# Two added pairs of one-column products in a two-layer decoder trunk: one in the first feed-forward, one in the convolution

## The chip, the cores and the metric

The kernel runs on one core of a Trainium2 chip. The metric is the time of one execution in microseconds, taken on the device. A core has TensorE (matmuls, "PE" in the profile, with its weight loads listed apart as "PEld"), VectorE ("DVE"), ScalarE ("ACT"), GpSimd ("POOL") and SyncE ("SP", which here issues the loads from memory). They run beside each other and wait for each other through semaphores. On TensorE every product is two instructions: a weight load, which puts a block of up to 128 columns into the array, and a matmul, which streams the other operand through it.

## What is computed

Two decoder layers over 256 positions and a model width of 1024, all in 32-bit floating point, about 150 MB of weights read once. Layer 0 mixes by attention, layer 1 by a short gated convolution, and each then has a gated feed-forward of width 2816:

```python
for i in range(DEPTH):                                   # DEPTH = 2
    mod = sc @ w_ada[i] + b_ada[i]                       # shifts, scales, gates
    sh_m, sc_m, g_m, sh_f, sc_f, g_f = jnp.split(mod, 6, axis=-1)
    h = modulate(x, norm_mix[i], sh_m, sc_m)
    y = moba_attention(...) if i % 2 == 0 else short_conv(...)
    x = x + g_m[:, None, :] * y
    h = modulate(x, norm_ffn[i], sh_f, sc_f)
    x = x + g_f[:, None, :] * swiglu(h, w_gate_up[i], w_down[i])

def short_conv(h, w_in, conv_w, w_out):
    b_gate, c_gate, u = jnp.split(h @ w_in, 3, axis=-1)
    u = c_gate * u
    up = jnp.pad(u, ((0, 0), (2, 0), (0, 0)))
    y = sum(conv_w[j] * up[:, j:j + S] for j in range(3))
    return (b_gate * y) @ w_out

def swiglu(h, w_gate_up, w_down):
    g, u = jnp.split(h @ w_gate_up, 2, axis=-1)
    return (jax.nn.silu(g) * u) @ w_down
```

## The kernel before

**Three products for one.** Every weight and every activation is split into a rounded part and a remainder (names ending in h and l), and a block of a matrix product is summed from three matmuls in the function mm3: high by high (line 248), high by low and low by high (lines 249 and 250). In the feed-forwards, the convolution and the output projections the weights are stationary: a matmul loads a block of 128x128 weights (wh or wl) and streams 256 positions of the activations (f0h, f0l and so on). Two of three neighbouring matmuls use the same stationary block, but each loads it anew. In the key and value projections of the attention the activations are the stationary operand and the weights stream.

**Chunks.** Weights arrive in chunks of 1 MB (256 output columns of all 1024 inputs) through five buffers; ScalarE rounds a chunk into wh (line 98), VectorE takes the remainder into wl (line 99), each in two halves and through three buffers. A chunk's load and split are put into the program two chunks ahead of its use. One chunk makes 48 matmuls: eight blocks of inputs, two halves of 128 columns, three products. In between, VectorE computes the modulation of later sublayers from chunks of w_ada (line 109).

**The stages.** A sublayer starts with the function raw_gemm: its first two weight chunks are multiplied with the not yet normalised activations (tiles raw_f, raw_m, 258 columns: 256 positions and two columns for the shift), 96 matmuls, so that TensorE has work while the norm is computed. In their midst stand small products for the norm (ms_n, rr_n). After it follow the ordinary chunks through feat_gemm: in a feed-forward ten times a gate chunk (tile pg) and an up chunk (tile pu), for j = 1 to 10, and then the down projection (op_d: 8 blocks of outputs, 22 blocks of inputs, three products, 528 matmuls); in the convolution one chunk for the B gate (pb) of j = 0, then for j = 1 to 3 one chunk each for pc, pu and pb, and then the output projection (op_co, 192 matmuls).

**The pair that is already there.** raw_gemm ends with a call of settle: two matmuls with a stationary block of 128x128 ones in bf16 and one streamed column, into a PSUM tile of its own that nothing reads. There are three such pairs: settle_f in each feed-forward, settle_m in the convolution.

**What sets the order.** The first stage, up to the queries and two of the key chunks, is written out by hand. For the rest a scheduler of the framework places each engine's instructions; on TensorE it follows the program's order, apart from the small products of the norm and the attention. PSUM tiles are of three kinds: "gemm" with four buffers, "alt" and "misc" with two each; settle takes its tile from "misc".

Of the kernel before, what the change touches and what calls it, by code (L numbers as in the profile page):

```python
# [15 lines left out]
P = 128  # L16
# [17 lines left out]
def trunk_kernel(ctx: ExitStack, tc: tile.TileContext, x_t, cols_in, scale_in, shift_in, ada_in, qk_rows, kv_in, o_in,  # L34
                 in_in, out_in, gu_in, down_in, out_f):
    nc = tc.nc
# [7 lines left out]
    def ps_gemm(name):  # L44
        return psum.tile([P, 2, CW], F32, tag="gemm", name=name, bufs=4)

    def ps_misc(name):
        return psum.tile([P, 512], F32, tag="misc", name=name, bufs=2)
# [15 lines left out]
    one_b = const.tile([P, 1], BF16, name="one_b")  # L64
# [102 lines left out]
    def conv_col(j, k):  # L167
        return v_cols[:, 32 + j * KD + k:][:, :1]
# [62 lines left out]
    def produce(upto):  # L231
        while pos[0] < len(chunks) and pos[0] <= upto:
            ch = chunks[pos[0]]
            if ch[0] == "a":
                ada_piece(*ch[1:])
            else:
                ready[ch[1]] = prep(ch[2], ch[3], "_".join(map(str, ch[1])), ch[1] in first_two)
            pos[0] += 1

    def get(key):  # L240
        n = place[key]
        produce(order[min(n + AHEAD, len(order) - 1)])
        return ready.pop(key)


    def mm3(ps, lhs, rhs, first, last):
        (ah, al), (bh, bl) = lhs, rhs
        nc.tensor.matmul(ps, ah, bh, start=first, stop=False, skip_group_check=True)  # L248
        nc.tensor.matmul(ps, ah, bl, start=False, stop=False, skip_group_check=True)  # L249
        nc.tensor.matmul(ps, al, bh, start=False, stop=last, skip_group_check=True)  # L250

    def feat_gemm(parts, xs, nk):
        xh, xl = xs
        for k in range(nk):
            for ps, (wh, wl) in parts:
                for o in range(2):
                    cs = slice(o * P, (o + 1) * P)
                    mm3(ps[:, o], (wh[:, k, cs], wl[:, k, cs]), (xh[:, k], xl[:, k]),
                        k == 0 and o == 0, k == nk - 1)
# [128 lines left out]
    def split(dst, k, src, name, psum_src=False):  # L388
        nc.scalar.activation(dst[0][:, k], src, AF.Copy)
        nc.vector.tensor_sub(dst[1][:, k], src, dst[0][:, k].bitcast(F32))  # L390

    def settle(name):

        ps = ps_misc("settle_" + name)
        for i in range(2):
            nc.tensor.matmul(ps[:, i:i + 1], one_b.to_broadcast([P, P]), one_b, start=True, stop=True, skip_group_check=True)

    def raw_gemm(keys, norm, name):

# [27 lines left out]
    def ffn(l, norm, av, done):  # L427
        for j in range(KF // 2):
            if j == 0:
                (s, bs), (a, ba), hs = raw_gemm([("g", l, j), ("u", l, j)], norm, f"f{l}")  # L430
                for o in range(2):
                    nc.scalar.activation(s[:, o], s[:, o], AF.Silu, bias=bs[:, o:o + 1])
                    nc.vector.scalar_tensor_tensor(a[:, o], a[:, o], ba[:, o:o + 1], s[:, o], op0=ALU.add,
                                                   op1=ALU.mult)
            else:
                pg, pu = ps_gemm(f"pg_{l}_{j}"), ps_gemm(f"pu_{l}_{j}")
                feat_gemm([(pg, get(("g", l, j)))], hs, KD)
                feat_gemm([(pu, get(("u", l, j)))], hs, KD)
                s = tmp.tile([P, 2, S], F32, tag="s", name=f"s_{l}_{j}")
                nc.scalar.activation(s, pg, AF.Silu)  # L440
                a = tmp.tile([P, 2, S], F32, tag="a", name=f"a_{l}_{j}")
                nc.vector.tensor_mul(a, s, pu)
            split(av, slice(2 * j, 2 * j + 2), a, f"{l}_{j}")
        out_proj([[(("d", l, j, i), n) for i, n in enumerate((8, 8, 6))] for j in range(4)], av, l, G_F, done)
# [15 lines left out]
    def mod_columns(y, name):  # L460

        ps = ps_misc(f"mod_c_{name}")
        n = y.shape[1] // P
        for i in range(n):
            nc.tensor.matmul(ps[:, i:i + 1], y[:, i * P:(i + 1) * P], firsts, start=True, stop=True)
        return ps[:, :n]
# [71 lines left out]
    with tc.manual_schedule(engines={mybir.EngineType.PE, mybir.EngineType.DVE, mybir.EngineType.Activation}):  # L538
# [13 lines left out]
        for k in range(KD):  # L552
            nc.tensor.matmul(c_ps[k // 4][:, k % 4 * P:][:, :P], sc[:, k:k + 1].to_broadcast([P, P]), ident, start=True,
                             stop=True)
# [18 lines left out]
        ps = mod_columns(y, "sc0")  # L573
# [13 lines left out]
        for k in range(KD):  # L587
            n = k + 1
# [167 lines left out]
    zv, zraw = wide_pair("zv")  # L756
    n1 = Norm("n1", 1, SH_M, SC_M, zraw)
    ffn(0, n0, av, n1.take)


# [3 lines left out]
    for j in range(4):  # L764
        up = ups[j % 2]
        if j == 0:
            (cg, bc), (cu, bu), hs = raw_gemm([("cg", j), ("cu", j)], n1, "m1")
            for o in range(2):
                nc.scalar.activation(cg[:, o], cg[:, o], AF.Identity, bias=bc[:, o:o + 1])
                nc.vector.scalar_tensor_tensor(up[:, o, 2:], cu[:, o], bu[:, o:o + 1], cg[:, o], op0=ALU.add,  # L770
                                               op1=ALU.mult)
        else:
            pc, pu = ps_gemm(f"pc_{j}"), ps_gemm(f"pu_{j}")
            feat_gemm([(pc, get(("cg", j)))], hs, KD)
            feat_gemm([(pu, get(("cu", j)))], hs, KD)
            cg = tmp.tile([P, 2, S], F32, tag="s", name=f"cg_{j}")
            nc.scalar.activation(cg, pc, AF.Copy)
            with tc.high_priority(400):
                nc.vector.tensor_mul(up[:, :, 2:], cg, pu)
        pb = (ps_alt2 if j else ps_gemm)(f"pb_{j}")  # L780
        feat_gemm([(pb, get(("cb", j)))], hs, KD)
        y = tmp.tile([P, 2, S], F32, tag="a", name=f"y_{j}")
        with tc.high_priority(400):
            for o in range(2):
                k = 2 * j + o
                nc.scalar.activation(y[:, o], up[:, o, 0:S], AF.Copy, scale=conv_col(0, k))
            for i in (1, 2):
                for o in range(2):
                    nc.vector.scalar_tensor_tensor(y[:, o], up[:, o, i:i + S], conv_col(i, 2 * j + o), y[:, o],
                                                   op0=ALU.mult, op1=ALU.add)  # L790
        z = tmp.tile([P, 2, S], F32, tag="s", name=f"z_{j}")
        with tc.high_priority(400):
            nc.vector.tensor_mul(z, y, pb)
            split(zv, slice(2 * j, 2 * j + 2), z, f"z{j}")
# [6 lines left out]
    def store(k):  # L801
        if k >= KD - 2:
            nc.sync.dma_start(out_f[:, k], xT[:, k])
        elif k % 2:
            nc.sync.dma_start(out_f[:, k - 1:k + 1], xT[:, k - 1:k + 1])

    ffn(1, n2, av, store)


# [58 lines left out]
```

## Time and profile before

| | |
|---|---|
| median of three runs | 601.7 us (600.98 to 604.31) |
| the profiled execution | 601.54 us |
| its span, from the first to the last instruction | 599.8 us |
| TensorE, matmuls | busy 590.5 us, 98% of the span, 5044 in the records |
| VectorE | busy 455.2 us, 76% |
| ScalarE | busy 314.3 us, 52% |
| memory traffic | 156 MB, mean 260 GB/s |
| granted TensorE clock | 0.999 |

The profiled execution's own time is 1.74 us above its span, for what lies before the first and after the last instruction. A row of the instruction list gives a start, a duration, the engine, the line, and the tiles written and read. Matmuls are pipelined: one lasts about 0.28 us in the records, and the next starts about 0.12 us after it, so that the distance from start to start, not the duration, is what a matmul costs in a stream. A view by windows counts every instruction that reaches into a window, so the count holds two or three matmuls that only overlap its edges. A few per cent of matmul records can be missing from a trace.

### The profile page before, as it was taken

Reading aid. Unit: us, or ns where it says so; the run is one execution under the profiler, and the core shown is the slowest. Engines: PE = TensorE matmul, PEld = TensorE weight load, DVE = VectorE, ACT = ScalarE, POOL = GpSimd, SP = SyncE. Lnnn points to the kernel's source line nnn. Section 1 sums busy time; section 2 is a strip of 40 time slices with the busy share of each in tenths; the row PEclk is TensorE's granted clock in tenths of the full one; section 3 lists DMA queues with packets and bytes.
Section 4 is the critical chain, followed back from the end, with each engine's and each line's share of the span. In section 5 each row is a group of like instructions: output and inputs, shape, how many; then the busy total and the mean of one; then the engine's idle time right before and its main releaser. Section 6 shows DMA issues by size and latency. Waiting matters only on the chain.

```text
span 599.8 us, 12042 instructions
## 1 busy us (share of the span) xinstructions
PE 590.5 (98%) x5044; PEld 581.9 (97%) x5044; DVE 455.2 (76%) x719; ACT 314.3 (52%) x526; POOL 1.1 (0%) x8
## 2 busy tenths in 40 slices
PE   7999999999999999999999999999999999999997
PEld 6899999999999999999999999999999999999997
DVE  2788988998997887878878998559887566664440
ACT  3646898776644354444444744527744544443330
POOL 0000000000000000000000000000000000000000
PEclk9999999999999999999999999999999999999999
DMA  8799989856798899868996577634486675655400
GB/s 332 269 379 413 377 308 324 334 198 231 257 384 293 330 346 343 283 245 291 354 361 256 190 285 275 212 141 152 181 317 260 216 251 179 260 190 183 169 18 18
DMA packets 25109, 156.04 MB, mean 260 GB/s; under 512 B 2784, under 2 KB 3168, under 8 KB 8928
## 3 DMA queue, kind: packets, MB, share of 16 engines
q1 hardware_dynamic: 24912, 155.20, 69.8%
q8 instruction: 39, 0.64, 0.4%
q10 hardware_dynamic: 144, 0.08, 0.1%
q14 instruction: 14, 0.11, 0.1%
HBM read 154.22 MB, written 1.05 MB: 259 GB/s over the span
## 4 chain that ended last, share of the span: by engine, by line
PE 96%; ACT 2%; DMA 1%; DVE 0%; issue 0%
PE pu L249 7%; PE pu L248 7%; PE pu L250 7%; PE op_d L249 7%; PE op_d L250 7%; PE op_d L248 7%; PE pg L249 6%; PE pg L248 6%; PE pg L250 6%; PE pq L248 1%; PE op_o L248 1%; PE pq L249 1%; PE raw_f L248 1%; PE pb L248 1%; PE pb L249 1%; PE raw_f L249 1%
## 5 line engine op out<-in xcount | busy, mean ns | idle before, releaser
L109 DVE SCALAR_TENSOR_TENSOR prod<-wa,c_all 128x1024 f32<-128x1024 f32 x80 | 97.7, 1222 | 11.2 <-DMA wa<-in_ada_dram 10.0
L98 ACT ACTIVATE wh_d<-wf_d 128x1024 fp32r<-128x1024 f32 (+1 forms) x48 | 45.3, 981 | 67.0 <-issue 46.3
L99 DVE TENSOR_TENSOR wl_d<-wf_d,wh_d 128x1024 fp32r<-128x1024 f32 (+1 forms) x48 | 52.9, 1133 | 24.9 <-ACT wh_d L98 24.9
L98 ACT ACTIVATE wh_g<-wf_g 128x1024 fp32r<-128x1024 f32 x44 | 45.7, 1052 | 46.7 <-issue 46.7
L98 ACT ACTIVATE wh_u<-wf_u 128x1024 fp32r<-128x1024 f32 x44 | 44.5, 1051 | 47.9 <-issue 47.4
L99 DVE TENSOR_TENSOR wl_u<-wf_u,wh_u 128x1024 fp32r<-128x1024 f32 x44 | 52.3, 1221 | 16.4 <-ACT wh_u L98 16.3
L99 DVE TENSOR_TENSOR wl_g<-wf_g,wh_g 128x1024 fp32r<-128x1024 f32 x44 | 53.4, 1221 | 2.4 <-ACT wh_g L98 2.4
L249 PE MATMUL op_d<-a0l,wh_d 128*128 128x256 f32 x176 | 49.3, 280 | 0.0
L248 PE MATMUL op_d<-a0h,wh_d 128*128 128x256 f32 x176 | 49.1, 279 | 0.0
L250 PE MATMUL op_d<-a0h,wl_d 128*128 128x256 f32 x176 | 49.1, 279 | 0.0
L248 PE MATMUL op_d<-a1h,wh_d 128*128 128x256 f32 x176 | 48.6, 276 | 0.0
L249 PE MATMUL op_d<-a1l,wh_d 128*128 128x256 f32 x176 | 48.6, 276 | 0.0
L250 PE MATMUL op_d<-a1h,wl_d 128*128 128x256 f32 x176 | 48.6, 276 | 0.0
L249 PE MATMUL pg<-f0l,wh_g 128*128 128x256 f32 x160 | 44.8, 280 | 0.0
L249 PE MATMUL pu<-f0l,wh_u 128*128 128x256 f32 x160 | 44.8, 280 | 0.0
L248 PE MATMUL pg<-f0h,wh_g 128*128 128x256 f32 x160 | 44.7, 280 | 0.0
L250 PE MATMUL pg<-f0h,wl_g 128*128 128x256 f32 x160 | 44.6, 279 | 0.0
L248 PE MATMUL pu<-f0h,wh_u 128*128 128x256 f32 x160 | 44.6, 279 | 0.0
L250 PE MATMUL pu<-f0h,wl_u 128*128 128x256 f32 x160 | 44.6, 279 | 0.0
L248 PE MATMUL pg<-f1h,wh_g 128*128 128x256 f32 x160 | 44.2, 277 | 0.0
L249 PE MATMUL pg<-f1l,wh_g 128*128 128x256 f32 x160 | 44.2, 276 | 0.0
L250 PE MATMUL pg<-f1h,wl_g 128*128 128x256 f32 x160 | 44.2, 276 | 0.0
(297 smaller groups left out, 2031.7 us busy)
## 6 DMA issues: line engine op xcount, KB each, us to landing
wa<-in_ada_dram SPq DMA_DIRECT2D x40, 1024.0 KB, 5.8
wf_g<-in_gate_up_dram SPq DMA_DIRECT2D x22, 1024.0 KB, 4.9
wf_u<-in_gate_up_dram SPq DMA_DIRECT2D x22, 1024.0 KB, 4.9
wf_d<-in_down_dram SPq DMA_DIRECT2D x16, 1024.0 KB, 5.6
wf_d<-in_down_dram SPq DMA_DIRECT2D x8, 768.0 KB, 5.5
wa_sc<-in_scale_dram SPq DMA_DIRECT2D x8, 512.0 KB, 6.5
wa_sh<-in_shift_dram SPq DMA_DIRECT2D x8, 512.0 KB, 7.0
wf_qk<-in_qk_rows_dram SPq DMA_DIRECT2D x8, 512.0 KB, 7.3
```

What stands on the lines that cost most here:

```text
L98: nc.scalar.activation(wh[:, a:b], wf[:, a:b], AF.Copy)
L99: nc.vector.tensor_sub(wl[:, a:b], wf[:, a:b], wh[:, a:b].bitcast(F32))
L109: nc.vector.scalar_tensor_tensor(t, w, 1.0, c_all, op0=ALU.mult, op1=ALU.mult, accum_out=dst)
L248: nc.tensor.matmul(ps, ah, bh, start=first, stop=False, skip_group_check=True)
L249: nc.tensor.matmul(ps, ah, bl, start=False, stop=False, skip_group_check=True)
L250: nc.tensor.matmul(ps, al, bh, start=False, stop=last, skip_group_check=True)
```

## The change

The function settle gets a second argument, the number of stationary columns of its second product; it is 128 unless said otherwise. Two calls with 64 are added. One stands in the first feed-forward only, at j = 1, between the gate chunk and the up chunk. The other stands in the convolution at j = 1, after the B-gate chunk of j = 0 and before the first pc chunk. The three pairs inside raw_gemm stay as they are.

```diff
-    def settle(name):
+    def settle(name, m=P):
 
         ps = ps_misc("settle_" + name)
-        for i in range(2):
-            nc.tensor.matmul(ps[:, i:i + 1], one_b.to_broadcast([P, P]), one_b, start=True, stop=True, skip_group_check=True)
+        for i, n in enumerate((P, m)):
+            nc.tensor.matmul(ps[:n, i:i + 1], one_b.to_broadcast([P, n]), one_b, start=True, stop=True, skip_group_check=True)
...
                 feat_gemm([(pg, get(("g", l, j)))], hs, KD)
+                if l == 0 and j == 1:
+                    settle("u1", P // 2)
                 feat_gemm([(pu, get(("u", l, j)))], hs, KD)
...
             pc, pu = ps_gemm(f"pc_{j}"), ps_gemm(f"pu_{j}")
+            if j == 1:
+                settle("c1", P // 2)
             feat_gemm([(pc, get(("cg", j)))], hs, KD)
             feat_gemm([(pu, get(("cu", j)))], hs, KD)
```

On TensorE this is the place in the first feed-forward, between the last product of the gate chunk (tile pg_1) and the first of the up chunk (pu_1); one_b is the vector of ones:

```order
 L249 MATMUL pg_1_2004<-f0l,wh_g_1_1825 128x256
 L250 MATMUL pg_1_2004<-f0h,wl_g_1_1826 128x256
+L396 LDWEIGHTS one_b
+L396 MATMUL settle_u_2062<-one_b 128x1
+L396 LDWEIGHTS one_b
+L396 MATMUL settle_u_2062<-one_b 64x1
 L248 MATMUL pu_1_2005<-f0h,wh_u_1_1833 128x256
 L249 MATMUL pu_1_2005<-f0l,wh_u_1_1833 128x256
```

Two weight loads and two matmuls stand between products that followed each other directly before. The changed kernel's rows on TensorE in the convolution, between the B-gate chunk (pb) and the first C-gate chunk (pc):

```order
L250 MATMUL pb_4208<-m1h,wl_cb_4026 128x256
L396 LDWEIGHTS one_b
L396 MATMUL settle_c_4278<-one_b 128x1
L396 LDWEIGHTS one_b
L396 MATMUL settle_c_4278<-one_b 64x1
L248 MATMUL pc_4276<-m1h,wh_cg_4039 128x256
L249 MATMUL pc_4276<-m1l,wh_cg_4039 128x256
```

The same four rows again; no other row of TensorE, and none of the other engines, changes its place.

## The prediction

> **What bounds the kernel now.** I read the page first: the span, the engines' shares, and the chain that ended last.
>
> ```profile
> span 599.8 us, 12042 instructions
> PE 590.5 (98%) x5044; PEld 581.9 (97%) x5044; DVE 455.2 (76%) x719; ACT 314.3 (52%) x526; POOL 1.1 (0%) x8
> PE 96%; ACT 2%; DMA 1%; DVE 0%; issue 0%
> ```
>
> TensorE is the bound: 96% of the chain is its own. Then the waits of TensorE, to see whether anything holds it up where the change is made:
>
> ```profile
> PE c_ps L553 <- ACT sc L545: 1.8, 1, 1.8
> PE warm L527 <- DVE ident_r L539: 1.8, 1, 1.8
> PE pv L249 <- DVE wl_v L99: 0.6, 1, 0.6
> PE op_o L248 <- ACT ovh L389: 0.5, 1, 0.5
> ```
>
> These are the longest. All lie in the opening and the attention; in the feed-forwards and the convolution TensorE waits for nobody. There the time is the number of matmuls times the distance from one start to the next. So I took the windows view over three long steady stretches, with TensorE alone: the first feed-forward, the convolution, the second feed-forward. The columns are the window, its length, the busy time with the count of matmuls, the granted clock, the DMA share and GB/s.
>
> ```profile
> 150.00:320.00 170.00, 170.00 (x1446) 1.00 0.84 312
> 337.00:410.00 73.00, 73.00 (x622) 1.00 0.56 202
> 430.00:594.00 164.00, 164.00 (x1450) 1.00 0.54 191
> ```
>
> This is the finding on which everything rests. A matmul of 0.28 us reaches over a window's edge, so some 2.4 of each count (0.28 divided by the spacing) belong outside: 170.00/1443.6 = 117.8 ns, 73.00/619.6 = 117.8 ns, 164.00/1447.5 = 113.3 ns. The same instruction, 128x128 by 256 columns, at the same granted clock of 1.00, has **two steady spacings**, 4.5 ns apart. The first feed-forward and the convolution run at the wide one, the second feed-forward at the narrow one, and each holds its own for its whole length, over every buffer of weights. The two feed-forwards are the same program, so size, operands and buffers do not choose it. What does stands at its beginning, and the timeline of TensorE shows both beginnings, first feed-forward, then second (start, duration):
>
> ```profile
> 147.46 0.28 PE L250 MATMUL raw_f<-a0h,wl_u 128*128 128x258 f32 x1
> 147.58 0.20 PE L396 MATMUL settle_f<-one_b 128*128 128x1 bf16 x2
> 147.64 0.36 PE L248 MATMUL pg<-f0h,wh_g 128*128 128x256 f32 x1
> 147.84 0.28 PE L249 MATMUL pg<-f0l,wh_g 128*128 128x256 f32 x1
> 147.96 0.28 PE L250 MATMUL pg<-f0h,wl_g 128*128 128x256 f32 x1
> ...
> 427.31 0.28 PE L250 MATMUL raw_f<-a1h,wl_u 128*128 128x258 f32 x1
> 427.43 0.20 PE L396 MATMUL settle_f<-one_b 128*128 128x1 bf16 x2
> 427.50 0.36 PE L248 MATMUL pg<-f1h,wh_g 128*128 128x256 f32 x1
> 427.69 0.28 PE L249 MATMUL pg<-f1l,wh_g 128*128 128x256 f32 x1
> 427.81 0.28 PE L250 MATMUL pg<-f1h,wl_g 128*128 128x256 f32 x1
> ```
>
> A pair of short products interrupts the stream; the next product starts early, then waits for its weights, and the second one after the pair comes 0.20 us later in the first case, 0.19 us in the second. From then on the stream is wide in the one and narrow in the other. I read this as a lock: how weight loads and matmuls fall against each other when the stream restarts settles the spacing until something interrupts it again.
>
> **The change part by part.** It removes nothing and moves nothing. It adds two pairs, each into a stream that runs wide.
>
> *Price of a pair.* From the last product ahead of settle_f to the second one behind it pass 147.84 - 147.46 = 0.38 us, where two spacings of 0.118 would be 0.24: a pair costs 0.15 us, and this is the lower end, since both added loads and products must pass. A gain from the short products as such is excluded; they take TensorE's time. The second added load has 64 columns, which no row of the trace shows. The load timeline bounds it:
>
> ```profile
> 147.57 0.12 PEld L396 LDWEIGHTS <-one_b 128*128 128x128 bf16 x2
> 147.62 0.19 PEld L248 LDWEIGHTS pg<-f0h,wh_g 128*128 128x128 f32 x1
> 147.73 0.19 PEld L249 LDWEIGHTS pg<-f0l,wh_g 128*128 128x128 f32 x1
> ```
>
> Two loads of ones took 0.05 us to the next start, so about 0.03 each; a load of 128 columns of weights took 0.11. If the 64-column load were as slow as that, the pair would cost 0.08 more, 0.23. I take 0.17, nearer the lower end, for half of 0.11 is 0.055, some 0.02 to 0.03 above 0.03. Two pairs: 0.34 us, between 0.30 and 0.46.
>
> The Trainium skill's page "TensorE: Matmul & The Clock Gate" says under "Weight-path perf modes — Fast Weight Load (FWL) and DoubleRow" that the fast load is on only for 128 weights of a type other than FP32, and under "LDWEIGHTS (loading the stationary operand)" that a plain load takes its columns divided by 1.2 ns. By it the 64 columns would take an estimated 53 ns and the pair 0.17 us; no row here shows such a load.
>
> *What the restart is worth.* Behind the first added pair, up to the next interruption at the convolution's raw_gemm, stand 48 matmuls of pu at j = 1, 9 x 96 of j = 2 to 10, and 528 of op_d: 1440. Behind the second stand 9 x 48 = 432 and 192 of op_co: 624. If the restart falls into the narrow spacing, each saves 4.46 ns (170.00/1443.6 less 164.00/1447.5, unrounded): 6.42 us and 2.78 us. If not, it saves nothing, and only the price is left. There is no value between, unless a stream changes its spacing half way.
>
> *Does the rest keep up?* The narrow stream asks for weights 4% faster. The windows view with all engines shows the densest stretch of the first feed-forward and the same stretch of the second:
>
> ```profile
> 153.00:261.00 108.00, 108.00 (x919) 108.00 (x918) 92.52 (x122) 49.28 (x62) 0.00 (x0) 1.00 0.88 330
> 433.00:536.00 103.00, 103.00 (x911) 103.00 (x910) 69.22 (x78) 48.97 (x59) 0.00 (x0) 1.00 0.66 241
> ```
>
> VectorE is busy 92.52 of 108.00 us, DMA 0.88. A stretch shorter by 4%, 103.9 us, would need 89% and 0.92: under one, so I cost this at nothing. The cover is the two chunks that are split ahead (11 us of TensorE's work). If it were gone, the stretch could not shrink below the 92.5 us of VectorE or the 95 us of DMA (0.88 of 108), both under 103.9. A single late transfer could still make a wait, and a wait is a restart.
>
> *Does the restart fall narrow?* This is the step that the trace cannot price, only count. The three pairs that exist gave narrow once (second feed-forward) and wide twice (the first and the convolution's settle_m). Other restarts of the same kind of stream, weights stationary: behind the attention's small products, and behind a wait for weights:
>
> ```profile
> 115.58 0.38 PE L717 MATMUL po<-vp 128*128 128x128 f32 x2
> 115.72 0.36 PE L248 MATMUL op_o<-ovh,wh_o 128*128 128x256 f32 x1
> 115.92 0.28 PE L249 MATMUL op_o<-ovl,wh_o 128*128 128x256 f32 x1
> ...
> 118.87 0.28 PE L250 MATMUL op_o<-ovh,wl_o 128*128 128x256 f32 x1
> ...
> 53.92 0.38 PE L249 MATMUL pq<-m0l,wh_qk 128*128 128x256 f32 x1
> 54.14 0.28 PE L250 MATMUL pq<-m0h,wl_qk 128*128 128x256 f32 x1
> ...
> 56.52 0.28 PE L250 MATMUL pq<-m0h,wl_qk 128*128 128x256 f32 x1
> ```
>
> From 115.92 to 118.87 lie 25 steps, 118 ns each: wide. From 54.14 to 56.52 lie 21 steps, 113 ns each: narrow. Both spacings are open to a restart, then, also where no ones are involved. With the three pairs that makes two narrow of five, and op_o has more restarts like the one shown. So a count gives a third at most. Two things set the new pairs apart. The old ones are entered from raw_gemm's 258-column stream; both new ones are entered from a settled wide stream behind the same line, 250, so they should both do the same. And their second load is longer, so weight load and matmul resume at another distance than in the two cases that came out wide; that makes them another throw, not a repetition of one that failed. A stream that is already wide can lose nothing by another throw. I put narrow for both a little under one half.
>
> *Sum.* 601.54 (the profiled execution's own time, 0.16 below the median) - 6.42 - 2.78 + 0.34 = 592.68; against the median of the runs shown, 601.7, that is **592.8 us**.
>
> **The rivals.**
>
> *Neither restart falls narrow.* 601.7 + 0.34 = 602.0. For it: two of the three pairs, and the op_o restart. [...]
>
> *Only one of the two.* The feed-forward alone gives 601.7 - 6.42 + 0.34 = 595.6, the convolution alone 601.7 - 2.78 + 0.34 = 599.3. Against it: the equal entry of both. For it: settle_f in the two feed-forwards came out differently in spite of equal code.
>
> *The second feed-forward loses its narrow stream.* Its own settle_f is untouched, but it is one throw as well, and what runs into it is a convolution displaced by the change. It decides where the restart at 427.50 comes out 0.20 us long instead of 0.19: 1487 matmuls (10 x 96, less the first, and 528) at 4.46 ns are 6.6 us. With neither gain, 602.0 + 6.6 = 608.6, slower by 1.1%; with both gains 599.4. Against it: between the convolution and that pair stand two interruptions (ms_n, rr_n) which start the stream anew, and these are as before.
>
> **How the numbers follow.** Both narrow 0.45 (592.8); neither 0.25 (602.0); feed-forward alone 0.08 (595.6); convolution alone 0.05 (599.3); second feed-forward lost with no gain 0.10 (608.6); lost beside both gains 0.07 (599.4). What a measurement here can tell from no change is 0.5%, 3.0 us: below 598.7 is faster, 0.45 + 0.08 = 0.53; within it, 0.25 + 0.05 + 0.07 = 0.37; slower 0.10. Since cases of both signs share the chance, the likeliest one's own range is narrow: 591.7 to 593.3, from a price of 0.30 to 0.46, the runs' scatter below the median, and up to 1 us if the raw products behind a narrow stream (96 each, at about 0.12 us) came closer too. The range that leaves out only the 608.6 goes from 591.5 to 602.7.
>
> **What would show it.** In the changed kernel's windows the first feed-forward from 154 us on should hold a matmul per 113.3 ns, about 1440 in 163 us, and the convolution the same from 335 us on, while the second feed-forward stays at 113.3. The second product behind each added pair should start 0.19 us or a little more after the first. Wide streams there (117.8) and a median of 602 would show the restart step wrong; narrow ones with waits of TensorE for wl tiles would show the cover wrong; 117.8 in the second feed-forward would show the last rival. The span should change by TensorE's spacing alone.

## The result, and the profile after

| | before | after |
|---|---|---|
| median | 601.36 us (600.33 to 604.31, 6 runs) | 607.96 us (607.50 to 609.05, 6 runs) |
| ratio after to before | | 1.0101, interval 1.0076 to 1.0127 |
| span of the profiled execution | 599.8 us | 606.0 us |

The changed kernel is slower by 1.0%. The forecast was 592.8 us; the outcome is the rival that ended on the other side (608.6 us). The page of the changed kernel looks as before, TensorE is still busy for 98% of the span:

```profile
span 606.0 us, 12050 instructions
PE 596.8 (98%) x5048; PEld 588.0 (97%) x5048; DVE 455.1 (75%) x719; ACT 314.3 (52%) x526; POOL 1.1 (0%) x8
```

Where the time went shows in the view by windows, TensorE alone, over the same three stretches as before (us, busy us, instructions that reach into the window, granted clock, DMA share, GB/s):

```profile
150.00:320.00 170.00, 170.00 (x1445) 1.00 0.84 314
337.00:410.00 73.00, 73.00 (x621) 1.00 0.56 202
430.00:594.00 164.00, 164.00 (x1395) 1.00 0.54 191
```

The first feed-forward (1446 before, 1445 now) and the convolution (622, 621) hold as many products as before, so both stayed at 117.8 ns. The second feed-forward held 1450 and now holds 1395 in the same 164 us, at the same clock: (164.00 / 1392.6) = 117.8 ns instead of 113.3. Nothing was added there. Its 1487 products at 4.46 ns are 6.6 us, which is more than the whole difference of the spans (6.2 us). The two pairs add 0.67 us, as the next rows show, and the opening was shorter in this execution: the first settle_f began at 146.48 us, where it was 147.58 before. So 599.8 + 6.6 + 0.67 - 1.10 = 606.0, the span.

The rows of TensorE and of its weight loads around the added pair in the first feed-forward of the changed kernel:

```profile
152.16 0.28 PE L250 MATMUL pg<-f0h,wl_g 128*128 128x256 f32 x1
152.29 0.30 PE L396 MATMUL settle_u<-one_b 128*128 128x1 bf16 x2
152.51 0.39 PE L248 MATMUL pu<-f0h,wh_u 128*128 128x256 f32 x1
152.74 0.28 PE L249 MATMUL pu<-f0l,wh_u 128*128 128x256 f32 x1
```

```profile
152.28 0.21 PEld L396 LDWEIGHTS <-one_b 128*128 128x128 bf16 x2
152.51 0.19 PEld L248 LDWEIGHTS pu<-f0h,wh_u 128*128 128x128 f32 x1
```

From the last product of pg to the second of pu pass 0.58 us, where two spacings are 0.24: the pair costs 0.34, not 0.17. The row of two short products lasts 0.30 us where the old pair's lasted 0.20, and the next product starts 0.22 us behind its beginning instead of 0.07. In the trace's nanoseconds the load of 64 columns starts 109 ns behind the load of 128 and the next load of 128 another 120 ns behind that, while the two loads of the old pair are 15 ns apart. Around the convolution's pair the products start 108 ns (first short one to second), 120 and 222 ns apart, so that pair costs 0.34 us as well.

And the place where the second feed-forward starts, behind its own settle_f, which the change doesn't touch:

```profile
426.92 0.28 PE L250 MATMUL raw_f<-a1h,wl_u 128*128 128x258 f32 x1
427.04 0.20 PE L396 MATMUL settle_f<-one_b 128*128 128x1 bf16 x2
427.10 0.36 PE L248 MATMUL pg<-f1h,wh_g 128*128 128x256 f32 x1
427.30 0.28 PE L249 MATMUL pg<-f1l,wh_g 128*128 128x256 f32 x1
427.42 0.28 PE L250 MATMUL pg<-f1h,wl_g 128*128 128x256 f32 x1
```

Before, the second product of pg came 0.19 us after the first (427.50 to 427.69), now 0.20 us (427.10 to 427.30). The steps of more than eighty products ahead of this are the same to the nanosecond in both traces; then come 40, 25, 200, 114 ns before and 39, 25, 201, 118 now. Up to the first narrow or wide step the two traces differ by a nanosecond at most, and behind it 6.6 us hang on the spacing. That nanosecond is no sign of which it will be: in two of the kernels below (8 instructions in the opening, 128 columns in all products) the steps were 39, 25, 201 as now, and 113 followed.

### The profile page after: what moved, and what is told of

It is laid out like the page before. It is cut to its first block, busy times and chain, and to the rows that moved or that the text cites. A ratio compares the mean times of both kernels' runs of the same rounds, so it can differ in the third digit from the quotient of the medians.

```text
span 606.0 us, 12050 instructions
## 1 busy us (share of the span) xinstructions
PE 596.8 (98%) x5048; PEld 588.0 (97%) x5048; DVE 455.1 (75%) x719; ACT 314.3 (52%) x526; POOL 1.1 (0%) x8
## 4 chain that ended last, share of the span: by engine, by line
PE 96%; ACT 2%; DMA 1%; DVE 0%; issue 0%
PE pu L248 7%; PE pu L249 7%; PE pu L250 7%; PE op_d L248 7%; PE op_d L249 7%; PE op_d L250 7%; PE pg L248 6%; PE pg L249 6%; PE pg L250 6%; PE pq L248 1%; PE pq L249 1%; PE op_o L248 1%; PE raw_f L248 1%; PE op_o L250 1%; PE raw_f L249 1%; PE op_co L250 1%
## 5 line engine op out<-in xcount | busy, mean ns | idle before, releaser
L249 PE MATMUL pu<-f1l,wh_u 128*128 128x256 f32 x160 | 44.8, 280 | 0.0
```

## Experiments

### Which part of the change does it

Four kernels separate the parts. The first two leave out one added pair each:

```diff
 # first: the pair in the first feed-forward alone
+                if l == 0 and j == 1:
+                    settle("u1", P // 2)
 # second: the pair in the convolution alone
+            if j == 1:
+                settle("c1", P // 2)
```

> The pair in the first feed-forward alone, none in the convolution. Theory 1 (the restart behind the second feed-forward's own settle pair is decided by what the stream brings from before, and both added pairs push it): a shift of the convolution by 0.3 us is already enough, second feed-forward at 117.8 ns, about 608 us. Theory 2 (only the convolution's pair, which is nearer, matters): second feed-forward stays at 113.3 ns and the time is 601.4 + 0.33 = 601.7 us. Both expect the first feed-forward at 117.8 ns behind the pair, as in the changed kernel.

> The pair in the convolution alone. Theory 1: as with either pair, second feed-forward at 117.8 ns, about 608 us. Theory 2: the convolution's pair alone does it, also about 608 us. If the second feed-forward stays at 113.3 ns here (601.7 us), it is the first feed-forward's pair that counts, or both together.

The third adds as many TensorE instructions as the change, but in the opening:

```diff
-        keep_warm(8)
+        keep_warm(12)
```

> The kernel before with four more warm-up products (8 more TensorE instructions, as many as the two pairs are) in the opening, where TensorE waits for transfers anyway; nothing is added to any of the three streams. If it is the place of the later instructions in TensorE's instruction stream that flips the restart, the second feed-forward goes to 117.8 ns here too, about 608 us. If it is a pair's disturbance of the running stream, it stays at 113.3 ns, 601.4 us within the scatter. If the outcome is a matter of chance for each program, either can come.

The fourth is the change with 128 columns in both products of both added pairs:

```diff
-                    settle("u1", P // 2)
+                    settle("u1", P)
-                settle("c1", P // 2)
+                settle("c1", P)
```

> The changed kernel with 128 columns in both products of the two added pairs. By the survey, where a 128/128 pair never gave a narrow stream behind a wide one, both streams stay wide; the price of a pair is 0.15 us instead of the 0.33 of the 128/64 pair, so 601.3 + 0.3 = 601.6 us if the second feed-forward's own settle pair still falls narrow, 608.2 if not. Phase theory: either, since the convolution ends at another phase. If it were the 64 columns of the convolution's pair that spoil the second feed-forward, narrow, 601.6.

| kernel | median, us | ratio to before | second feed-forward |
|---|---|---|---|
| pair in the first feed-forward alone | 601.87 | 1.0011 (0.9989 to 1.0034) | see below |
| pair in the convolution alone | 608.29 | 1.0123 (1.0106 to 1.0140) | 117.8 ns |
| 8 instructions in the opening | 601.14 | 0.9995 (0.9981 to 1.0009) | 113.3 ns |
| both pairs with 128 and 128 columns | 601.58 | 0.9999 (0.9980 to 1.0018) | 113.3 ns |

The window of the second feed-forward, first with the convolution's pair alone, then with the eight instructions in the opening, then with full columns:

```profile
430.00:594.00 164.00, 164.00 (x1395) 1.00 0.53 191
```

```profile
430.00:594.00 164.00, 164.00 (x1449) 1.00 0.53 191
```

```profile
430.00:594.00 164.00, 164.00 (x1450) 1.00 0.53 191
```

The profiled execution of the first kernel ran at a granted clock of 0.755, so its spacings can't be set beside the others; its median, 0.6 us above the 601.30 of before beside it, leaves room for the pair's 0.34 and none for 6.6. So the convolution's pair is the cause, alone and wholly. The place of instructions in TensorE's stream is not, and neither is a pair as such at that place: with 128 columns it leaves the second feed-forward narrow. What a pair of 64 columns does there must travel through 600 products, a raw stage and two other interruptions to reach settle_f. It isn't what such pairs do in general: eight profiled executions of later kernels have 128/64 pairs in the convolution too (elsewhere, with more behind them, or entered from another stream), and in all eight the second feed-forward was narrow from settle_f on.

### What an interruption leaves behind

The survey puts an interruption at each gap between chunks. The list is for a feed-forward, in order from u of j = 1 to u of j = 10; it has 19 gaps there, not 20 as the expectation counts, and 47 interruptions in all.

```diff
+    KINDS = [(P, P)] * 4 + [(P, P // 2)] * 4 + [(P,)] * 4 + [(P // 2,)] * 4 + [(P, P, P)] * 4
+    CONV_KINDS = [(P, P)] * 3 + [(P,)] * 3 + [(P, P, P)] * 3
```

> The kernel before with an interruption at each of the 20 gaps between chunks of both feed-forwards (four each of a pair of 128 and 128 columns, a pair of 128 and 64, a single 128, a single 64, three of 128) and at 9 gaps of the convolution (three each of a pair, a single, three of 128). Each shows which spacing the 48 products behind it take. If the form of the interruption sets it, the four of a form agree, in both feed-forwards; if the phase or the place sets it, forms are mixed and the same gap of the two feed-forwards need not agree. 49 interruptions at 0.15 to 0.33 us cost 7 to 16 us; with all 4100 products behind them narrow it would be 18 us less than all wide, so the whole lies between 595 and 625 us and the time itself tells nothing.

It ran 616.41 us. One window of 5 us behind one interruption of each form, first feed-forward (128/128; 128/64 entered from a wide stream; 128/64 entered from a narrow one; single 128; single 64; three of 128). About 45 instructions are wide, 46 to 47 narrow:

```profile
153.90:158.90 5.00, 5.00 (x45) 1.00 0.66 242
177.30:182.30 5.00, 5.00 (x46) 1.00 1.02 416
183.10:188.10 5.00, 5.00 (x47) 1.00 0.34 136
200.20:205.20 5.00, 5.00 (x45) 1.00 0.95 323
223.60:228.60 5.00, 5.00 (x45) 1.00 0.94 328
247.30:252.30 5.00, 5.00 (x45) 1.00 0.46 135
```

All eight 128/64 pairs were followed by a narrow stream, in both feed-forwards; all 39 others by a wide one. Equal draws do not give 8 of 8 beside 0 of 39, even though six of the eight were entered from a stream that was narrow already. But the form alone cannot be it either, since the changed kernel's two pairs are of that same form and both left a wide stream.

What differs is the stream that enters. A wide stream has a pattern of three: two steps of 117 to 118 ns and one that is longer by a nanosecond, always at the same of the three products of a block. The view of groups shows it without counting steps: the product behind the long step has a mean of 280 ns, the other two 279. In the survey the first 128/64 pair of each feed-forward was entered from a stream with the long step after the product of line 250 (mark 280 on line 248); the changed kernel's two were entered with it after line 248 (mark 280 on line 249). This became the phase theory: the entering pattern decides.

### The phase theory tested

Five kernels put the 128/64 pair, written (P, W) with W = 64, behind different forerunners, as lists of place and columns (u0_1: first feed-forward, ahead of u of j = 1; u1 and g1 are the second feed-forward's, cg, cu and cb the convolution's):

```diff
 # repeated
+    PAIRS = {"u0_1": (P, W), "g0_2": (P, W), "cg_1": (P, W), "cu_1": (P, W), "cb_1": (P, W)}
 # entered otherwise
+    PAIRS = {"u0_1": (P, P, P), "g0_2": (P, W), "cg_1": (P, P), "cu_1": (P, W), "u1_1": (P, W), "g1_2": (P, W)}
 # two more pairs in the second feed-forward
+    PAIRS = {"u0_1": (P, W), "cg_1": (P, W), "u1_1": (P, W), "g1_2": (P, W)}
 # three of 128 ahead, in each stream
+    PAIRS = {"u0_1": (P, P, P), "g0_2": (P, W), "cb_1": (P, P, P), "cg_2": (P, W), "u1_1": (P, P, P), "g1_2": (P, W)}
 # control
+    PAIRS = {"u0_1": (P, P), "g0_2": (P, W), "u1_1": (P, P), "g1_2": (P, W)}
```

> The changed kernel with the pair repeated at the next chunk borders: first feed-forward ahead of u and g (j = 1, 2), convolution ahead of the first C, U and B chunk (j = 1); second feed-forward untouched. Phase theory (what a 128/64 pair does depends on which of the three products of a block takes the longest step in the stream that enters it: entered with the longest step on line 250, or narrow, it leaves a narrow stream; entered with it on line 248, a wide one): the first pair of the first feed-forward leaves a wide stream with the longest step on line 250, as in the changed kernel, and the second pair a narrow one; first feed-forward from g of j = 2 on at 113.3 ns, 1391 products x 4.46 = 6.2 us less. In the convolution the first pair leaves the longest step on line 249, for which no case is known; open. Place theory (the 128/64 pairs of the survey came out narrow because of where they stood, j = 3 to 5): wide everywhere in the first feed-forward, as after one pair. Second feed-forward: either. Time by the phase theory with 5 x 0.33 = 1.65: 601.3 + 1.65 - 6.2 = 596.8, with the convolution narrow 594.6, and 6.6 more for either where the second feed-forward is wide; by the place theory 603 or 609.6.

> Other ways to bring the stream into the state from which the pair came out narrow. First feed-forward: three products of 128 columns ahead of u (j = 1), the 128/64 pair ahead of g (j = 2). Convolution: a pair of 128 and 128 ahead of the first C chunk, the 128/64 pair ahead of the U chunk. Second feed-forward: 128/64 pairs ahead of u (j = 1) and g (j = 2). Phase theory: wherever the first interruption leaves the longest step on line 250 (three of 128 did so twice, from a stream with it on line 248), the 128/64 pair behind it gives 113.3 ns; and the second feed-forward is narrow from j = 2 on whatever its own settle pair does, since a narrow stream stayed narrow through the pair 6 times of 6 and a wide one has two throws. Time: 601.3 + 4 x 0.33 + 0.17 + 0.15 - 6.2 (first feed-forward) - 2.6 (convolution) = 594.1. Place theory: no gain, and the second feed-forward loses what its pairs cost: 603 to 610.

> The changed kernel with two more 128/64 pairs, in the second feed-forward ahead of u (j = 1) and g (j = 2). Up to these the program is the changed kernel, so its stream enters the first of them wide with the longest step on line 248. Phase theory: the first pair leaves it wide but with another product longest, as it did three times from that state, or narrow; the second, entered with the longest step on line 250, makes it narrow: 1391 products x 4.46 = 6.2 us less than the changed kernel, 2 x 0.33 more, 608.0 - 6.2 + 0.7 = 602.5 us. If the spacing of a whole feed-forward is settled at its beginning (by where its data lies, or by what else runs), the pairs change nothing: 608.7 us.

> In each of the three streams three products of 128 columns, and one chunk later the 128/64 pair: in both feed-forwards ahead of u (j = 1) and g (j = 2); in the convolution ahead of the B chunk of j = 1 and the C chunk of j = 2, behind the place where the two last runs had TensorE wait for weights. Phase theory: three of 128 left the longest step on line 250 six times of nine, and from a stream with it on line 248 three of three; a 128/64 pair entered so gives 113.3 ns (four of four that ran on undisturbed). So all three streams are narrow behind the pair, in every execution, unless TensorE waits for weights in the midst: 601.5 - 6.2 - 2.1 (480 products) + 3 x 0.5 + 0.2 (one chunk of the second feed-forward wide) = 594.9 us. Chance theory (each interruption is an independent draw, narrow about one time in three): the executions scatter between 595 and 609 with the median near 602.

> In both feed-forwards a pair of 128 and 128 ahead of u (j = 1) and the 128/64 pair ahead of g (j = 2); nothing in the convolution. Phase theory: what the second pair leaves goes by the stream that enters it. Where that has its longest step on line 248 (as a pair of 128 left it in the first feed-forward of the run before with full columns), wide; where on line 250 (as a pair of 128 left it behind a narrow stream in the survey's second feed-forward), narrow. So the first feed-forward most likely stays wide and the second is narrow again from j = 2 on: 601.5 + 2 x 0.48 + 0.2 = 602.7 us. Place or form theory (a 128/64 pair ahead of g, j = 2, is narrow as in the last two kernels that had it): both narrow, 596.5 us.

The control is the sharpest. Both feed-forwards hold the same forms at the same places. The groups of TensorE in the 5 us ahead of the 128/64 pair, first feed-forward, then second (mean ns behind the comma), and the windows behind the pair:

```profile
L249 PE MATMUL pu<-f0l,wh_u 128*128 128x256 f32 x15 | 4.2, 280 | 0.0
L250 PE MATMUL pu<-f0h,wl_u 128*128 128x256 f32 x15 | 4.2, 279 | 0.0
L248 PE MATMUL pu<-f0h,wh_u 128*128 128x256 f32 x15 | 4.2, 279 | 0.0
```

```profile
L248 PE MATMUL pu<-f1h,wh_u 128*128 128x256 f32 x15 | 4.2, 280 | 0.0
L250 PE MATMUL pu<-f1h,wl_u 128*128 128x256 f32 x15 | 4.2, 279 | 0.0
L249 PE MATMUL pu<-f1l,wh_u 128*128 128x256 f32 x15 | 4.2, 279 | 0.0
```

```profile
159.00:310.00 151.00, 151.00 (x1284) 1.00 0.86 318
442.00:590.00 148.00, 148.00 (x1308) 1.00 0.55 198
```

The mark is on line 249 in the first and on 248 in the second; the first stays wide (117.8 ns), the second goes narrow (113.3). The time, 602.88 us, is the 602.7 that the theory gave; place or form would have given 596.5. With the pair repeated, the first feed-forward did what was expected: wide behind the first pair, narrow behind the second.

```profile
154.00:159.00 5.00, 5.00 (x44) 1.00 0.71 262
160.00:310.00 150.00, 150.00 (x1326) 1.00 0.88 324
```

Over all profiled executions, without the one at a granted clock of 0.755 and one pair that was cut short by a wait, with the mark read ahead of each 128/64 pair:

| stream that enters | followed by narrow | followed by wide |
|---|---|---|
| wide, mark on line 248 | 13 | 2 |
| wide, mark elsewhere or none | 0 | 13 |
| narrow | 14 | 0 |

So the rule holds in 40 of 42 cases; 11 of them (the changed kernel, the convolution's pair alone and the survey) are those that it was drawn from. The two exceptions (in the runs with halved transfers and with the convolution alone, below) carry the same mark as the 13, so the mark isn't the whole state; what lies under the trace's whole nanoseconds isn't seen.

The times, against forecasts that assumed the rule:

| kernel | forecast, us | median, us | executions, us | ratio to before |
|---|---|---|---|---|
| repeated | 596.8 | 597.27 | 594.97 to 605.71 | 0.9937 (0.9908 to 0.9967) |
| entered otherwise | 594.1 | 599.97 | 595.23 to 604.95 | 0.9949 (0.9921 to 0.9977) |
| two more pairs | 602.5 | 595.43 (2 executions) | 594.41 to 596.46 | 0.9901 (0.9877 to 0.9926) |
| three of 128 ahead | 594.9 | 600.29 | 596.83 to 602.02 | 0.9979 (0.9958 to 1.0001) |
| control | 602.7 | 602.88 | 600.78 to 606.01 | 1.0018 (0.9993 to 1.0043) |

The spacings followed the theory and the times did not always. The kernel with two more pairs was no test of what it was made for: its first feed-forward came out narrow at settle_f already, and so did its second. In the kernel entered otherwise the convolution's pair was cut short by a wait for weights. And three of 128 ahead gave narrow streams in all three stages of the profiled execution (1326 in 150 us, 435 in 49 us, 1326 in 150 us), yet 598.0 us in that execution and 600.29 as the median, not 594.9. Two questions followed: does the program fix what happens, and what eats the gain?

### Does the program fix the outcome

The changed kernel and the kernel with two more pairs were run once more, unchanged.

> The changed kernel once more. If what a stream locks into is fixed by the program, the first feed-forward and the second are wide again, 608.0 us in each execution, as in six of six; if it differs from execution to execution or from chip to chip, times near 602 or 595 turn up.

> The kernel with the two further pairs in the second feed-forward once more. Up to the second feed-forward its program is the changed kernel's, yet its first feed-forward came out narrow from settle_f on. If the program fixes the outcome, 595.4 us again in each execution; if the execution does, the first feed-forward is wide here as in the changed kernel and the time is 602.5 us, or both turn up.

The changed kernel gave 608.88 us (608.06 to 611.17, ratio 1.0127, 1.0094 to 1.0160), again wide in all three stages (1395 products in the window of the second feed-forward). The other gave 600.19 us (ratio 0.9961, 0.9932 to 0.9991), its executions from 595.26 to 605.26. In its profile the first feed-forward and the second were again narrow from settle_f on, although the program up to there is the changed kernel's. So the times of before and of the changed kernel, where TensorE never waits in the streams, repeat; those of kernels in which it waits scatter from one execution to the next. Why settle_f of the first feed-forward came out narrow in three profiles (two of this kernel, one of the kernel entered otherwise) and wide in all others isn't explained; the programs up to there are the same.

### What eats the gain of a narrow first feed-forward

In the repeated kernel's profile TensorE waits 2.43 us behind the first feed-forward. VectorE's rows, then TensorE's:

```profile
315.37 1.23 DVE L109 SCALAR_TENSOR_TENSOR prod<-wa,c_all 128x1024 f32<-128x1024 f32 x1 [2.56 <-DMA wa<-in_ada_dram]
...
319.94 2.36 DVE L99 TENSOR_TENSOR wl_cu<-wf_cu,wh_cu 128x1024 fp32r<-128x1024 f32 x2
```

```profile
321.21 0.39 PE L250 MATMUL raw_m<-zvh,wl_cu 128*128 128x258 f32 x1 [2.43 <-DVE wl_cu L99]
```

VectorE waits 2.56 us for a chunk of w_ada, does that, the remainder of cg and the second half of the chunk, and only then the remainder of cu that TensorE stands still for. Supply did not grow with demand, as the same stretch shows before and in the kernel with three of 128 ahead:

```profile
160.00:315.00 155.00, 155.00 (x1319) 155.00 (x1318) 130.47 (x180) 69.55 (x90) 0.00 (x0) 1.00 0.87 324
```

```profile
160.00:315.00 155.00, 155.00 (x1370) 155.00 (x1370) 131.26 (x183) 71.69 (x92) 0.00 (x0) 1.00 0.87 322
```

TensorE takes 4% more weights, the transfers bring the same 322 to 324 GB/s at a DMA share of 0.87, and VectorE's waits for w_ada between 150 and 330 us grow from 8.6 us to 18.2. Those waits alone show little: in kernels whose first feed-forward is wide they go from 6.1 us (the convolution's pair alone) to 15.4 (128 columns in all products), and the control, wide there too, has TensorE wait behind it, 0.8 us for ms_n and 0.3 for wl_cu. Nor is it shown what sets the 322 GB/s: over five microseconds of the survey the transfers brought 416. Halving the w_ada transfers was to show whether bytes are all (the two kernels leave half of each later w_ada chunk unread and use the other half twice):

```diff
-        w = load(ada_in[l, part, i], 2 * D, ...)
+        w = load(ada_in[l, part, i][:, :D], D, ...)
 ...
-            ada_sum(mcol(l, part, 2 * i + n), w[:, n], ...)
+            ada_sum(mcol(l, part, 2 * i + n), w, ...)
```

> The kernel with three short products and a 128/64 pair in each stream, but every later w_ada transfer is half as large (0.5 MB instead of 1 MB, and the half that came is used for both columns; the modulation of the later sublayers is left wrong, the amount of arithmetic stays). Supply theory (the narrow first feed-forward runs ahead of the transfers: VectorE waits for a w_ada chunk, the remainder wl_cu is queued behind that on VectorE, TensorE waits for wl_cu; this gives back part of the gain and scatters the executions): without 14 MB of transfers the waits of TensorE around 318 to 344 us vanish, and all executions lie near 601.5 - 6.2 - 2.1 + 1.7 = 594.9 us. Chance theory: still scattered from 596 to 602.

> The kernel before with the same halved w_ada transfers, for the difference: TensorE waited for nothing in its streams there, so the time stays at 601.5 us, within 1 us; or goes to 595 or 608 where one of the two feed-forwards locks otherwise.

Without interruptions 601.77 us (ratio 1.0010, 0.9992 to 1.0028), as expected. With them 600.75 us (0.9989, 0.9978 to 1.0000): the scatter went, 600.02 to 601.83, but not to 594.9. The convolution was wide this time (one of the two exceptions, 2.1 us). VectorE still waited for w_ada, 23.7 us in all, though each transfer was half as large (18.3 us without interruptions, where TensorE waited for nothing). TensorE's wait for wl_cu shrank to 0.1 us, its two for the norm's sums (ms_n, 0.33 and 0.81 us) were there, and the granted clock fell to 0.79 in the 5 us around them. So this run doesn't settle how much of the loss is bytes.

Three more runs start the narrow stream elsewhere: the two pairs of the first feed-forward alone; the first feed-forward in its second half, with the convolution; the convolution alone.

```diff
 # first feed-forward alone
+    PAIRS = {"u0_1": (P, W), "g0_2": (P, W)}
 # late start
+    PAIRS = {"u0_6": (P, P, P), "g0_7": (P, W), "cb_1": (P, P, P), "cg_2": (P, W)}
 # convolution alone
+    PAIRS = {"cg_1": (P, P, P), "cu_1": (P, W)}
```

> Only the two 128/64 pairs of the first feed-forward (ahead of u, j = 1, and of g, j = 2) that came out narrow in the run with repeated pairs; nothing in the convolution and in the second feed-forward. Phase theory: first feed-forward narrow from j = 2 on wherever the first of them leaves the longest step on line 250; second feed-forward as it falls. 601.5 + 0.66 - 6.2 = 596.0 us without waits, 597 to 600 with the 1.4 to 4 us of waits for transfers that the other narrow runs had behind the first feed-forward.

> The first feed-forward made narrow only in its second half: three of 128 columns ahead of u (j = 6), the 128/64 pair ahead of g (j = 7); in the convolution three of 128 ahead of the B chunk of j = 1 and the 128/64 pair ahead of the C chunk of j = 2; second feed-forward untouched. Supply theory (the transfers of the first feed-forward bring no more bytes a second to a faster TensorE, so a narrow stream eats its lead over the transfers, 4.5 ns a product, and waits when the lead is gone): 912 narrow products eat 4.1 us instead of 6.2 to 6.7, so waits are fewer than in the runs that were narrow from j = 2 on, and the executions scatter less: 601.5 - 4.1 - 2.1 + 2 x 0.5 = 596.3 us plus at most 1 us of waits. If the scatter comes from a different lock in each execution, it is as wide as before, 596 to 602.

> The convolution alone, where the transfers were busy for 0.65 of the time: three of 128 columns ahead of the first C chunk (j = 1), the 128/64 pair ahead of the U chunk behind it. Phase theory: narrow behind the pair, 528 products x 4.46 = 2.4 us less, 0.5 more for the short products: 601.5 - 1.9 = 599.6 us if the second feed-forward's own settle pair falls narrow, 606.2 if wide. Supply theory: no waits here, so little scatter.

The first feed-forward alone gave 599.02 us (0.9947, 0.9925 to 0.9969), within the 597 to 600 forecast for a gain with waits. Its profiled execution was the slowest of its eleven (606.34 us): TensorE waited for weights at 293, 311, 322 and 325 us, 2.14 us for wl_d at 311 and 2.44 for wl_cu at 325.

The late start gave 599.38 us (0.9977, 0.9954 to 0.9999). In its profile TensorE waits for nothing from 215 to 331 us, so the stage from settle_f to settle_m takes 184.45 us where 188.0 + 0.5 - 4.1 = 184.4 was due: in this execution the shorter narrow stream kept its whole gain. But the waits turned up in the convolution instead (0.66, 0.59 and 0.33 us from start to start), and the executions scatter as widely as before, 596.79 to 602.89; that the scatter would shrink was wrong.

The convolution alone gave 602.26 us (1.0018, 1.0001 to 1.0035). Its pair was entered with the mark on line 248 and yet left a wide stream, the second exception; so there was no gain, only the price of the short products: an estimated 0.5 us by their rows, and 1.0 us between the medians. (576 products stand behind that pair, not the 528 of the expectation.)

The mean granted clock was measured for every execution, and it parts them. Of the executions of the six kernels above with full transfers and a first feed-forward that is narrow in the profile, 36 had a mean of 0.999 or 1.000 and a median of 597.3 us, and 31 had 0.997 or less and a median of 601.7. In the profiles the lowered clock is a stretch at half rate behind a wait: 0.50 from 322.4 to 329.1 us in the repeated kernel, 0.50 from 328.3 to 331.6 with the convolution alone, an estimated 3.0 and 1.5 us lost, with products 0.215 us apart instead of 0.12. So much of the scatter goes with a lowered clock. How the 4.4 us divide between clock and waits isn't separated here.

The best that was measured with enough executions is the repeated kernel, 597.27 against 601.69 us. It beats the kernel before by 0.6%, and doesn't hold that in each execution.

## Why the prediction was wrong

- **What bounds the kernel: right.** The span followed TensorE's spacing alone; no wait in the streams of the changed kernel.
- **"Does the restart fall narrow": wrong, in its chance and in its kind.** A little under one half was given to both falling narrow; both fell wide, at 117.8 ns, and the 9.2 us of gain didn't come. That both "should both do the same" held. But "another throw" was the mistake: what a 128/64 pair leaves is mostly settled by the pattern of the stream that enters, and both were entered from a pattern (mark 280 on line 249) out of which this pair gave a wide stream every time, 11 of 11 over all runs. The pattern could have been read from the profile of before, in the group rows' means; that it mattered could not.
- **"A stream that is already wide can lose nothing": true of that stream**, and it stayed as it was. The stream that lost was another.
- **The last rival, "the second feed-forward loses its narrow stream", 0.10: this is what happened**, with its price right (6.6 us) and its place (the restart behind settle_f). The sign given for it, a restart 0.20 us long instead of 0.19, was there but tells nothing: 0.20 also stood ahead of narrow streams (201 ns, then 113). Behind a 128/64 pair it was 222 ns whether the stream came out narrow (in the survey) or wide (in the changed kernel's convolution). The argument against it, that ms_n and rr_n "start the stream anew", is the other step that failed: they don't wipe out what came before. The convolution's pair alone turned the second feed-forward wide (1395 products in its window, four executions of four at 607.7 us or more), and the same pair with 128 columns did not. What carries the memory across them stays open.
- **The price of a pair, 0.17 us between 0.15 and 0.23: mis-sized by half**, 0.34 measured, outside its bounds. The term took half of a 128-column load for 64 columns. What counts is not the load's own length but that a load of 64 columns doesn't follow one of 128 until 109 ns later, nor is it followed for another 120. By the Trainium skill's page "TensorE: Matmul & The Clock Gate", section "LDWEIGHTS (loading the stationary operand)", the 64 columns were an estimated 53 ns; the rows of the changed kernel show twice that on either side.
- **The cover, "I cost this at nothing": not put to the test by the change, and wrong.** Where the first feed-forward was made narrow, weights came late. The step from a DMA share of 0.88 to one of 0.92 took what was left to one for slack, but the same stretch ran at 0.87 whether TensorE asked for 4% more or not. Kernels with a narrow first feed-forward came to medians of 597.3 to 600.3 us (one, in two executions, to 595.4), so the 592.8 would hardly have held in full with two narrow streams either; what the lost part is made of isn't settled.
- **The sum, remade with what was measured:** 601.36 + 6.6 + 0.67 = 608.6, against 607.96; the same kernel run once more gave 608.88. That this is also the rival's 608.6 is in part luck: its two pairs were priced too low by 0.33 us, and its base was 0.34 us too high.

## What to carry to other kernels

A stream of equal products can run at more than one steady spacing, and an interruption chooses which for everything up to the next, and can change what a later one chooses; before adding one, look for streams elsewhere that are at the better spacing by luck and will be thrown again. When a small edit moves a whole stage by a fixed per cent, compare the windows stage by stage before looking at the edit itself. And a share below one is no proof of slack: here a DMA share of 0.87 stayed at 0.87 when TensorE took 4% more.

## What the runs showed of the hardware that was not expected

- **The spacing is locked, and the lock has a memory.** The same product runs at 117.8 or 113.3 ns at a granted clock of 1.00, over more than a thousand products without change. A narrow stream stayed narrow through a 128/64 pair 14 times of 14, and a single 128, a pair or three of 128 put between the chunks always left a wide one (31 of 31 in the survey), also behind a narrow. A wide stream comes in three patterns, told apart by which of three products has 280 ns.
- **A short product with 64 stationary columns, between products with 128, costs 0.32 us alone; a pair of one with 128 and one with 64 costs 0.34, and a pair with 128 and 128 only 0.15** (in the survey a single of 64 took 209, 120 and 222 ns from start to start, a single of 128 took 121, 39 and 200).
- **The clock can drop after a short wait.** In the repeated kernel, five microseconds each, TensorE alone:

```profile
315.00:320.00 5.00, 3.78 (x33) 1.00 0.49 177
320.00:325.00 5.00, 3.24 (x19) 0.73 0.90 333
325.00:330.00 5.00, 5.00 (x26) 0.58 0.92 356
330.00:335.00 5.00, 5.00 (x44) 1.00 0.61 206
```

Behind the wait of 2.43 us the granted clock falls to 0.73 and 0.58, and raw products start 0.215 us apart instead of 0.12; the lowered clock costs an estimated 3.0 us (6.7 us at 0.50, as above), more than the wait itself. In other profiles a wait of about 1 us was followed by a lower clock (0.82, the convolution alone) or not (1.00, three of 128 ahead), and one of 2.14 us was not either (1.00 from 310 to 320 us, the first feed-forward alone). The Trainium skill's page "TensorE: Matmul & The Clock Gate" says under "Part 1: The HAM clock gate" that the half rate comes back after an idle window of about 3.4 us; here no single wait was that long.
